# Layer 1's mixer of a two-layer trunk: query, key and output-gate projections as seven half-size products per pair, kept in DRAM, and four recurrences that run afterwards

## The chip, the core and the metric

The kernel runs on one core of one Trainium2 chip, as one program in one launch. The metric is the device time of that launch in microseconds (us). It counts the matmuls of the tensor engine (PE), its weight loads (PEld), the vector engine (DVE), the scalar engine (ACT), GpSimd (POOL) and the DMA queues, which are mostly issued by the sync engine (SP). Host work is not counted; numpy only lays the inputs out.

## The reference, cut to what matters

Two layers work on 1024 frames of width 1024. Layer 0 mixes with an attention and a pooling, layer 1 with gated linear attention, and each is followed by a feed-forward block. The change lies in layer 1's mixer (`odd_mixer`), which computes, with the batch left out:

```python
def odd_mixer(h, w_in, w_a2, b_a, o_gain, w_out):
    proj = h @ w_in
    q, k, v, r, a_low = jnp.split(proj, ...)        # 512, 512, 1024, 1024, 16 columns
    q = q.reshape(b, s, 4, 128) * 128 ** -0.5
    k = k.reshape(b, s, 4, 128)
    v = v.reshape(b, s, 4, 256)
    log_alpha = log_sigmoid(a_low @ w_a2 + b_a) / 16.0
    o = gated_linear_attention(q, k, v, log_alpha)
    o = rms_norm(o, o_gain).reshape(b, s, 1024)
    return (o * silu(r)) @ w_out

def step(state, inp):                               # once for each chunk of 64 frames
    q_c, k_c, v_c, decay_c = inp
    state = decay_c[..., None] * state + einsum('bchk,bchv->bhkv', k_c, v_c)
    return state, einsum('bchk,bhkv->bchv', q_c, state)
```

There are four heads, sixteen chunks, and a state of 128 x 256 for each head. `h` is `rms_norm(x, mix_norm_odd)`.

## The kernel before, in words

**Layout.** Activations lie transposed: 128 features on the partitions, 1024 frames along the free dimension, so `x` is eight tiles `x[0]` to `x[7]`. Every dense product is in three parts: each fp32 operand is split into a high and a low part (`hi`, `lo`, of type fp32r), and a product is hi x hi + hi x lo + lo x hi (`mm3`, lines 150 to 156, which the profile shows as L152, L154 and L156). A projection tile of 128 output features takes 8 input blocks x 2 halves of the frames x 3 = 48 matmuls of 128x512 (`linear`). A split is an ACT copy (L138) and a DVE subtraction (L139).

**What sets the order.** The order of PE is written out by hand: the program order of the matmuls is PE's order. The other engines and SP's DMA queue are put in order by the compiler, from a simulated time line with program order as priority. Within a recurrence a `Filler` hands out pieces of other generators, each `yield` saying how many us of PE work it stands for.

**The seven products.** The two feed-forward blocks (`ffn`) already use a scheme after Winograd and Strassen. Two projection tiles (a "pair") share 2x2 blocks of weights and activations; instead of eight products of half size there are seven (`Pair.P1` to `P7`, each 12 matmuls of 128x512, L937), and sums of weight halves (`sums`, L906 to L909) and of activation halves (`rsums`, L959 to L962, then `rblock`, which splits them) are made beforehand. `us` and `tm` are tiles for the pair's outputs and intermediate results. `scaled` (L965) multiplies by the norm's reciprocal.

**Layer 1's mixer before** (from L1187 on) uses no such scheme. While the last tiles of layer 0's down projection are added up, `Norm.add` (L255 to L271) splits `x[m]` into `h_hi`, `h_lo`, and head 0's key tile is projected between them (`onward`). Then, head by head:

- values `v_proj` (L1266 to L1268: 8 frame blocks of 24 matmuls of 128x256), evacuated by one ACT and one DVE instruction each (L1272, L1273);
- `q_proj`, `k_proj`, `r_proj` (`linear` again), and the gates (`gates`: one small matmul for each half, L1304, then ACT's Abs, Sigmoid, Ln, sixteen DVE scans, L1318, and Exp);
- `keys`: multiply by the decay, transpose on PE (L1334), split;
- `recur`: eight steps of two chunks. A step has six small matmuls for the state update (L1371 to L1373), DVE's new state (L1378), its split (L1380 on ACT, L1381 on DVE), and three matmuls that read the state of the step before (L1354 to L1356), whose result ACT copies out (L1358, L1359) and squares (L1361). One eighth of an `r_proj` tile fills each step;
- `gated`: root, reciprocal, eight scalings (ACT L1398, POOL L1400), PE transposes (L1409), product with the gate (L1412) and split (L1414, L1415), with the rest of the projections beside it;
- the output projection of that head is added to `x` (`accumulate`, L859), for the last head inside `ffn`.

Everything of the mixer stays in SBUF: `h` in the 16 tiles of `hpool`, `x` in eight of the 11 slots of `xpool`. Weights pass through one raw tile (`wraw`) and two pairs of split tiles (`whi`, `wlo`) in `wpool`. The four PSUM tags `lin`, `z`, `t` and `d` have two banks each.

## Time and profile before

| what | value |
|---|---|
| time, median of 3 runs | 2246.44 us |
| lowest and highest | 2243.03 and 2246.78 us |
| the profiled execution's own time | 2246.21 us |
| span in the profile, first to last instruction | 2244.2 us |
| mean granted PE clock | 0.998 |
| layer 1's mixer, from the last head-0 key products to the first product of its `ffn` | 1128.15 to 1530.80 us of the span |
| HBM traffic | 159.98 MB read, 42.99 MB written |

"Busy" is the time in which an engine has at least one instruction under way. Matmuls overlap in the array, so the mean duration of a 128x512 matmul (about 0.39 us) is not the time that it costs: that is the distance from one start to the next, which comes out of a stretch of the trace divided by the matmuls in it. "Idle before" of a group is what its engine waited ahead of it, and an arrow names the instruction that ended the wait.

### The profile page before, as it was taken

The numbers are of one execution on the slowest core, as the hardware profiler recorded it, in microseconds if no ns is written. First come the engines' busy times: TensorE is split into PE (matmuls) and PEld (weight loads), VectorE is DVE, ScalarE is ACT, GpSimd is POOL, SyncE is SP. The second block draws the span as 40 slices with busy tenths as digits, with TensorE's granted clock in tenths as the row PEclk, the third lists the DMA queues.
The fourth block names the chain that finished last, engine by engine and source line by source line (L and its number), as shares of the span: only waits on it lengthen the run. The fifth ranks groups of instructions, "written<-read, shape, count | busy, mean of one in ns | idle before, by whom it ended". The sixth has DMA issues, their size and how long they took to land.

```text
span 2244.2 us, 27677 instructions
## 1 busy us (share of the span) xinstructions
PE 2208.7 (98%) x10648; PEld 1815.5 (81%) x10648; DVE 1590.4 (71%) x2239; ACT 1010.5 (45%) x1488; POOL 229.4 (10%) x184
## 2 busy tenths in 40 slices
PE   8999989999999999999999999999999999999999
PEld 7888868788888888888887878887888888888887
DVE  5687788788888889554546555547888888885543
ACT  6666666454444444221256263537544444442210
POOL 2230120000000001421000000001000000013210
PEclk9999999999999999999999999999999999999999
DMA  4132441433333336421101111105333333364312
GB/s 149 52 106 81 118 140 51 146 100 112 107 106 108 113 113 225 160 98 53 31 20 48 29 47 38 48 29 164 91 108 107 113 109 103 109 226 148 110 40 75
DMA packets 71908, 220.50 MB, mean 98 GB/s; under 512 B 8400, under 2 KB 11088, under 8 KB 71776
## 3 DMA queue, kind: packets, MB, share of 16 engines
q1 hardware_dynamic: 64576, 203.00, 28.1%
q0 software_dynamic: 7200, 15.73, 3.9%
q8 instruction: 84, 1.38, 0.3%
q14 instruction: 48, 0.39, 0.1%
HBM read 159.98 MB, written 42.99 MB: 90 GB/s over the span
## 4 chain that ended last, share of the span: by engine, by line
PE 88%; DVE 4%; ACT 3%; DMA 2%; issue 1%; SPq 0%; POOL 0%; DVEq 0%; ACTq 0%; POOLq 0%
PE lin L937 15%; PE z L937 10%; PE lin L152 6%; PE lin L154 5%; PE lin L156 5%; PE t L937 5%; PE d L937 5%; PE z L152 4%; PE z L154 4%; PE z L156 4%; PE t L152 3%; PE t L154 3%; PE t L156 2%; PE d L154 2%; PE d L152 2%; PE d L156 2%
## 5 line engine op out<-in xcount | busy, mean ns | idle before, releaser
L138 ACT CAST whi<-wraw 128x1024 fp32r<-128x1024 f32 (+2 forms) x102 | 104.2, 1023 | 341.1 <-PE d L154 182.0
L139 DVE TENSOR_TENSOR wlo<-wraw,whi 128x1024 fp32r<-128x1024 f32 (+1 forms) x88 | 128.5, 1461 | 44.5 <-ACT whi L138 43.8
L1010 ACT ACTIVATE c<-u,prm 128x1024 f32<-128x1024 f32 x88 | 109.3, 1244 | 106.2 <-DVE u L965 89.8
L1174 POOL TENSOR_TENSOR act<-a,act 128x1024 fp32r<-128x1024 f32 x40 | 105.6, 2647 | 268.8 <-ACT act L1173 254.5
L152 PE MATMUL lin<-h_hi,whi 128*128 128x512 f32 x304 | 118.2, 427 | 7.2 <-ACT whi L138 6.1
L937 PE MATMUL d<-T,a 128*128 128x512 f32 x480 | 115.4, 389 | 0.0
L1011 DVE SCALAR_TENSOR_TENSOR c<-u,prm,c 128x1023 f32<-128x1023 f32 x88 | 112.2, 1277 | 3.7 <-ACT c L1010 3.6
L1013 DVE SCALAR_TENSOR_TENSOR c<-u,prm,c 128x1022 f32<-128x1022 f32 x88 | 113.7, 1294 | 0.1
L908 POOL DMA_DIRECT2D s<-s x40 | 34.4, 859 | 762.4 <-ACT s12h L916 619.1
L154 PE MATMUL lin<-h_lo,whi 128*128 128x512 f32 x304 | 108.7, 395 | 1.7 <-DVE h_lo L262 1.7
L965 DVE TENSOR_TENSOR u<-u,rstd_bc 128x512 f32<-128x512 f32 x160 | 109.3, 683 | 0.3
L156 PE MATMUL lin<-h_hi,wlo 128*128 128x512 f32 x304 | 108.3, 395 | 0.0
L859 DVE TENSOR_TENSOR x<-x,t 128x512 f32<-128x512 f32 x93 | 63.5, 683 | 59.7 <-PE t L156 59.7
L937 PEld LDWEIGHTS d<-T,a 128*128 128x128 f32 x480 | 90.1, 188 | 18.7
L937 PE MATMUL z<-blk,s34h 128*128 128x512 f32 x320 | 100.9, 397 | 0.0
L937 PE MATMUL z<-blk,s12h 128*128 128x512 f32 x320 | 100.9, 396 | 0.0
L937 PE MATMUL t<-blk,whi 128*128 128x512 f32 x320 | 99.6, 392 | 0.0
L937 PE MATMUL lin<-blk,whi 128*128 128x512 f32 x320 | 99.5, 392 | 0.0
L859 DVE TENSOR_TENSOR x<-x,d 128x512 f32<-128x512 f32 x93 | 63.4, 682 | 50.9 <-PE d L156 50.9
L937 PE MATMUL lin<-T,s12h 128*128 128x512 f32 x320 | 99.3, 391 | 0.0
L937 PE MATMUL lin<-T,s34h 128*128 128x512 f32 x320 | 99.3, 391 | 0.0
L859 DVE TENSOR_TENSOR x<-x,z 128x512 f32<-128x512 f32 x78 | 53.3, 683 | 60.0 <-PE z L156 60.0
(444 smaller groups left out, 6336.7 us busy)
## 6 DMA issues: line engine op xcount, KB each, us to landing
wraw<-in_wup SPq DMA_DIRECT2D x44, 512.0 KB, 3.6
act<-c SPq DMA_DIRECT2D x44, 512.0 KB, 2.6
wraw<-in_wdn SPq DMA_DIRECT2D x44, 512.0 KB, 4.0
raw_g<-in_wup SPq DMA_DIRECT2D x40, 512.0 KB, 3.7
a<-act SPq DMA_DIRECT2D x40, 512.0 KB, 4.4
s<-in_wup SPq DMA_DIRECT2D x40, 256.0 KB, 2.6
s<-s POOLq DMA_DIRECT2D x40, 256.0 KB, 4.2
xs<-x SPq DMA_DIRECT2D x16, 512.0 KB, 3.4
```

The source lines that it names most:

```text
L138: S.copy(hi[:, cs], raw[:, cs])
L139: (eng or V).tensor_tensor(lo[:, cs], raw[:, cs], hi[:, cs].bitcast(F32), op=ALU.subtract)
L152: PE.matmul(out[i], wh, ah[i], start=first, stop=False)
L154: PE.matmul(out[i], wh, al[i], start=False, stop=False)
L156: PE.matmul(out[i], wl, ah[i], start=False, stop=last)
L859: V.tensor_tensor(x[m][:, cs], x[m][:, cs], pss[m][i], op=ALU.add)
L937: PE.matmul(ps, w, m, start=first and k == 0 and n == 0, stop=k == 3 and n == 2, skip_group_check=True)
L965: V.tensor_tensor(dst, dst, rstd_bc[:, cs], op=ALU.mult)
L1010: S.activation(c, u, AF.Identity, scale=pcol(b + 2), bias=pcol(b + 3))
L1011: V.scalar_tensor_tensor(c[:, 1:], u[:, :T - 1], pcol(b + 1), c[:, 1:], op0=ALU.mult, op1=ALU.add)
L1013: V.scalar_tensor_tensor(c[:, 2:], u[:, :T - 2], pcol(b), c[:, 2:], op0=ALU.mult, op1=ALU.add)
L1174: G.tensor_tensor(t[1], a32, t[0].bitcast(F32), op=ALU.subtract)
```

## The change

Layer 1's mixer is put in a new order, and most of its projections are computed in another way.

- `winograd(...)` is taken out of `ffn` as a function, with the same operations, and is used a second time.
- `norm` becomes a `NormBlocks`: each `x[m]` is stored to DRAM (`xs`), and split in four blocks by half of the frames; `x[0..3]` are scaled in place. With `by_dma=False` the squares are added by DVE.
- Head 0's key (still with `linear_b` in `onward`) and query stay plain, 48 matmuls each. The other three keys, three queries and the eight tiles of `r` are seven pairs.
- First come head 0's values, with `rsums` and `rblock` (16 sums, 16 splits of 128x512) beside them, then head 0's query, the gates of heads 0 and 1, the second half of the frames of head 2's and head 3's values, the gates of heads 2 and 3, all of head 1's values; then the seven pairs in a row, with `keys`, `queries` and `r_gate` beside them.
- All results go to DRAM tiles (`qd`, `kd`, `vhd`, `vld`, `rd`, `ed`) and are fetched again by `fetch_half` and `fetch_r` when a recurrence needs them. `x` leaves its slots and is loaded again by `reload_x` in the second recurrence.
- Then the four recurrences run one after another. Their fillers are: in recurrence 0 the first half of head 2's values (four pieces, one of them ahead of it), in recurrence 1 that of head 3's, in recurrences 2 and 3 the output projection of heads 0 and 1 together (16 pieces, two of them ahead), and then that of head 2. Head 3's is left to `ffn`, as before.

The loops around the pairs and the recurrences, cut:

```diff
-    norm = Norm(C_MIXO, lambda: slot(F32, "nacc"), lambda: slot(F32, "nsq"), V)
+    norm = NormBlocks("m", C_MIXO, lambda: slot(F32, "nacc"), lambda: slot(F32, "nsq"), by_dma=False)
...
+    PAIRS = ([(wok[1], wok[2]), (wok[3], woq[1]), (woq[2], woq[3])]
+             + [(wor[2 * hd], wor[2 * hd + 1]) for hd in range(GH)])
+    w = winograd(gp, norm, lambda i: PAIRS[i], us, tm, t1=lambda: slot(R32, "T1"))
...
+    for k in range(4):
+        w.rsums(k)
+        for n in ("T4", "T2", "T3", "T1"):
+            w.rblock(n, k)
+        next(v)
...
+    v = v_proj(3, SECOND, w3, lambda a: (slot(R32, "vst"), w.a22), v_store(3), vtags)
+    next(v)
+    w1 = v_weights(1)
+    next(v)
+    gates((2, 3), ("lin", "z"), [(w.raw_g, w.s34), (w.s12, lz)])
+    run(v)
+    v = v_proj(1, [*SECOND, *FIRST], w1, lambda a: (slot(R32, "vst"), slot(R32, "vst")), v_store(1), vtags)
+    for _ in range(4):
+        next(v)
+    loads = (w.load_g, w.load_a, w.load_s4)
+    for ld in loads:
+        ld(0)
+    w.split_a22()
+    w.sums(0)
...
+    run(v)
...
+    for i in range(N):
+        nx, further = i + 1 < N, i + 2 < N
+        if i == 0:
+            p = w.Pair(0)
+            p.P1()
+        ua, ug = p.ua, p.ug
+        if i == 1:
+            ks[1], ks[2] = keys(1, us[0]), keys(2, us[1])
+            next(ks[1])
...
+        p.P5()
+        if nx:
+            w.sums(i + 1)
+            w.split_a11(i + 1)
...
+        p.P4()
+        p.D21()
...
+            p = w.Pair(i + 1)
+            p.P1()
+        pq.P3()
...
+        if i >= 3:
+            for f, u in enumerate((ua, ug)):
+                r_gate(i - 3, f, u)
...
+    fetch_half(0, 0)
+    fetch_half(0, 1)
+    fl = Filler()
+    fl.add(early(2, wf))
+    fl.fill(2.6)
+    nxt = {}
+    o0 = recur(0, fl, 10.4, {3: lambda: fetch_half(1, 0), 4: lambda: nxt.update(w=v_weights(3)),
+                             5: lambda: (fetch_half(1, 1), fetch_r(0))})
+    g0 = gated(0, *o0)
+    next(g0)
+    fl.add(early(3, nxt["w"]))
+
+    def in1(j):
+        if j == 2:
+            mixt[0] = next(g0)
+        elif j == 3:
+            fetch_half(2, 0)
+            ow[0] = [out_w(0, hpool, ("h", "h"), nb=16), out_w(1, hpool, ("h", "h"), nb=16)]
+        elif j == 4:
+            run(g0)
+        elif j == 5:
+            fetch_half(2, 1)
+            fetch_r(1)
+            reload_x()
+        elif j == 6:
+            ow[1] = [out_w(2), out_w(3)]
+
+    o1 = recur(1, fl, 16.0, {j: (lambda j=j: in1(j)) for j in range(NT)})
+    g1 = gated(1, *o1)
+    next(g1)
+    mixt[1] = next(g1)
+    run(g1)
+    fl.add(outputs_of(ow[0] + ow[1], mixt[0] + mixt[1]))
+    fl.fill(5.2)
...
+    keep(fl)
+    o2 = recur(2, fl, 18.0, {j: (lambda j=j: in2(j)) for j in range(NT)})
+    g2 = gated(2, *o2)
+    next(g2)
...
+    o3 = recur(3, fl, 20.0, {j: (lambda j=j: in3(j)) for j in range(NT)})
+    g3 = gated(3, *o3)
+    next(g3)
+    del fl.drain
+    fl.drain()
+    o = outputs_of(ow[2], mixt[2])
     for _ in range(4):
-        next(rr)
...
+        next(o)
+    mixt[3] = next(g3)
+    for _ in range(4):
+        next(o)
+    run(g3)
+    run(o)
```

The functions that these lines call, where they are new or different:

```diff
+    def gates(hds, tags, tiles):
+        for hd, tag, (l1, l2) in zip(hds, tags, tiles):
...
+                PE.matmul(gp_, gin["w"][:, hd * GDK:(hd + 1) * GDK], gin["a"][:, cs], start=True, stop=True)
+                S.activation(l1[:, cs], gp_, AF.Abs, bias=ba)
+                V.tensor_scalar(l2[:, cs], gp_, ba, 0.0, op0=ALU.add, op1=ALU.min)
+        for f in (AF.Sigmoid, AF.Ln):
+            for l1, _ in tiles:
+                S.activation(l1, l1, f)
...
+        for hd, (l1, _) in zip(hds, tiles):
+            S.activation(l1, l1, AF.Exp, scale=1.0 / TAU)
+            S.activation(decs[hd], decs[hd], AF.Exp, scale=1.0 / TAU)
+            dma(ed[hd], l1)
...
+    def early(hd, wt):
+        return v_proj(hd, FIRST, wt, lambda a: (ring("vh")(), ring("vl")()), v_store(hd), ltags)
...
+    def outputs_of(ws, acts):
+        for m in range(KT):
+            sl = slice(m * P, (m + 1) * P)
+            for cs in HALVES:
+                ps = bank(next(ltags))
+                for k, (wk, ak) in enumerate(zip(ws, acts)):
+                    mm3([ps], (wk[0][:, sl], wk[1][:, sl]), ([ak[0][:, cs]], [ak[1][:, cs]]),
+                        k == 0, k == len(ws) - 1)
+                yield 0.65 * len(ws)
+                V.tensor_tensor(x[m][:, cs], x[m][:, cs], ps, op=ALU.add)
+
+    def keep(fl):
+        fl.drain = lambda: None
```

`ffn` keeps its own calls and takes the functions from `winograd`. The scan, the state update and the read of a recurrence are the same instructions as before, with other operand tiles.

More of the change, by code (lines that the diff above doesn't have):

```diff
@@ L865, in accumulate, with winograd @@
                 after(m)
-    def ffn(layer, nm, after, ow, mixt, onward=None):
-        ev = ExitStack()
-        up = ev.enter_context(tc.tile_pool(name=f"up{layer}", bufs=1, reuse_waits="tile"))
+    def winograd(up, nm, wt, us, tm, t1=lambda: hpool.tile([P, T], R32, tag="h", name="blk")):
         T0, T1 = HALVES
@@ new lines, in onward, with dt @@
+    def onward(load):
+        return linear_b(load(wok[0]), lambda cs, ps: V.tensor_tensor(
+            k0[0][:, cs], ps, rstd_bc[:, cs], op=ALU.mult), "lin", late=late)
+    ffn(0, n0, lambda m: norm.add(m, x[m]), ws, [mix[k] for k in last], onward)
+    def dt(name):
+        return dram.tile([P, T], F32, tag=name, name=name)
+    qd, kd, vhd, vld = ({(hd, a): dt(f"{n}{hd}_{a}") for hd in range(GH) for a in range(2)}
+                        for n in ("qd", "kd", "vhd", "vld"))
+    rd = {(hd, f): dt(f"rd{hd}_{f}") for hd in range(GH) for f in range(2)}
@@ new lines, in r_gate @@
+    def r_gate(hd, f, u):
+        S.activation(u, u, AF.Silu)
+        dma(rd[hd, f], u)
+    k0.append(w.s34)
+    v0to = [(w.s12h, w.s12l), (w.s34h, w.s34l)]
+    v = v_proj(0, range(NT), ahead, lambda a: v0to[a], v_store(0), itertools.cycle("td"))
+    next(v)
+    norm.stats("z")
+    next(v)
+    next(v)
+    norm.spread(itertools.repeat("z"))
+    for f in late:
+        f()
+    dma(raw0["k"], w.s34)
+    for k in range(4):
[3 more added lines that the diff above has]
+        next(v)
@@ new lines, in trunk_kernel @@
+    qw = [w.s12h, w.s12l]
+    qraw = wpool.tile([P, T], F32, tag="wraw", name="wraw", bufs=1)
+    dma(qraw, woq[0])
+    next(v)
+    w.split(*qw, qraw)
+    run(v)
+    g = gate_inputs()
+    next(g)
+    q32 = slot(F32, "q32")
+    q = linear_b(tuple(qw), lambda cs, ps: V.tensor_tensor(q32[:, cs], ps, rstd_bc[:, cs], op=ALU.mult), "z")
+    for _ in range(4):
+        next(q)
+    run(g)
+    for _ in range(3):
+        next(q)
+    lz = slot(F32, "l2")
+    gates((0, 1), ("lin", "td"[0]), [(w.raw_g, w.s34), (w.s12, lz)])
@@ L1346, in recur, with fetch_r @@
+    sr = {}
+    def fetch_r(hd):
+        for f in range(2):
+            sr[hd, f] = op.tile([P, T], F32, tag="r", name="r32", bufs=2)
+            dma(sr[hd, f], rd[hd, f])
+    def recur(hd, fl, us_, at):
+        dec = decs[hd]
+        oraw = []
         ss = small.tile([P, NT], F32, tag="ss", name="ss")
```

450 lines of the change are left out of this document (261 added, 189 removed).

## The prediction

> **What bounds the kernel now.** I read the page first, then the chain of waits, then the windows of layer 1's mixer, then the groups of ACT and DVE inside it.
>
> ```profile
> span 2244.2 us, 27677 instructions
> PE 2208.7 (98%) x10648; PEld 1815.5 (81%) x10648; DVE 1590.4 (71%) x2239; ACT 1010.5 (45%) x1488; POOL 229.4 (10%) x184
> PE 88%; DVE 4%; ACT 3%; DMA 2%; issue 1%; SPq 0%; POOL 0%; DVEq 0%; ACTq 0%; POOLq 0%
> ```
>
> PE is busy in 98% of the span and is 88% of the chain that ends last. So a PE instruction less is time saved, as long as PE finds its operands, and a PE wait added is time lost. The windows say where PE waits today (columns: length, then busy time and count of PE, PEld, DVE, ACT, POOL, then clock, DMA share, GB/s).
>
> ```profile
> 1106.00:1128.15 22.15, 22.15 (x96) 17.81 (x96) 20.23 (x24) 13.10 (x14) 0.62 (x1) 1.00 0.00 0
> 1128.15:1135.15 7.00, 5.86 (x26) 4.43 (x25) 7.00 (x8) 5.20 (x6) 0.33 (x1) 1.00 0.00 0
> 1135.15:1162.90 27.75, 27.75 (x214) 26.75 (x213) 7.34 (x14) 10.35 (x22) 0.00 (x0) 1.00 0.01 1
> 1237.00:1240.80 3.80, 1.63 (x8) 0.98 (x6) 3.77 (x6) 0.88 (x1) 0.13 (x1) 1.00 0.18 22
> 1240.00:1245.00 5.00, 4.20 (x12) 3.34 (x13) 5.00 (x19) 1.05 (x1) 0.00 (x0) 0.68 0.38 107
> 1284.60:1307.80 23.20, 23.11 (x122) 16.51 (x122) 17.02 (x37) 15.97 (x44) 0.00 (x0) 1.00 0.16 46
> 1516.80:1530.80 14.00, 13.36 (x65) 10.43 (x64) 5.46 (x9) 11.53 (x21) 1.85 (x4) 1.00 0.44 151
> 1530.80:1547.10 16.30, 13.46 (x51) 10.02 (x50) 14.89 (x22) 10.86 (x16) 0.88 (x1) 0.90 0.42 145
> 1128.15:1530.80 402.65, 398.38 (x2222) 332.15 (x2221) 219.34 (x413) 199.67 (x379) 8.24 (x21) 1.00 0.14 41
> ```
>
> In 402.65 us PE idles 4.3 us. A recurrence (1284.60 to 1307.80 is head 1's) is filled without a gap: 23.2 us.
>
> **The change, part by part.** First what a matmul costs, from three stretches with one kind of work: one `r` tile (48 matmuls, counted by their weight loads), one pair of the feed-forward block (84), four value steps.
>
> ```profile
> 1318.70:1329.60 10.90, 10.90 (x49) 8.96 (x48) 2.44 (x4) 3.42 (x4) 0.00 (x0) 1.00 0.18 48
> 1661.30:1680.70 19.40, 19.40 (x85) 15.77 (x84) 16.79 (x21) 8.84 (x10) 0.86 (x1) 1.00 0.38 109
> 1267.20:1278.70 11.50, 11.50 (x98) 11.50 (x97) 1.93 (x4) 1.90 (x4) 0.00 (x0) 1.00 0.01 1
> ```
>
> *Products.* Fourteen plain tiles go, 14 x 10.90 = 152.6 us; seven pairs come, 7 x 19.40 = 135.8 us. That is **-16.8 us**. Values, outputs, transposes, gate matmuls and the recurrences' own matmuls stay the same in number.
>
> *Waits that go.* Head 0's output products wait today for a query's evacuation, and the clock falls after it:
>
> ```profile
> PE z L152 <- DVE q L1228: 2.2, 1, 2.2
> PE d L152 <- DVE x L859: 2.1, 1, 2.1
> ```
>
> 2.2 us and (1 - 0.68) x 5 = 1.6 us, **-3.8 us**: that place no longer exists. At the end of the mixer (1516.80 to 1547.10) PE idles 0.6 + 2.8 us and loses 0.10 x 16.3 = 1.6 us of clock, 5.0 in all, while DVE is busy 14.89 of 16.30 us with the last head's gating, weight splits and the first sums at once. In the new order 16 pieces of output products lie behind that gating's start, so DVE has it done earlier; the splits remain. Bounds 0 and -5.0; I take **-3.5**.
>
> *The blocks of the norm.* Eight `x[m]` get two half splits in place of a whole one. DVE had 20.23 busy of 22.15 us before 1128 and is full to 1135. Two 0.747 in place of one 1.28 is 0.2 us for each, 1.7 in all, partly hidden: **+0.5** (0 to 3).
>
> ```profile
> L305 DVE SCALAR_TENSOR_TENSOR blk<-x,prm,blk 128x512 fp32r<-128x512 f32 x16 | 11.6, 747 | 1.0 <-ACT blk L304 1.0
> L962 DVE SCALAR_TENSOR_TENSOR x<-x,prm 128x512 f32<-128x512 f32 x4 | 3.0, 742 | 0.0
> L917 DVE TENSOR_TENSOR T<-x,T 128x512 fp32r<-128x512 f32 x12 | 8.0, 675 | 0.0
> L1273 DVE SCALAR_TENSOR_TENSOR vl<-t,rstd_tok,vh 128x256 fp32r<-128x256 f32 x16 | 7.7, 483 | 32.6 <-ACT vh L1272 32.6
> ```
>
> *Sums beside head 0's values.* For each k DVE gets four sums and four splits, about 3 x 0.742 + 5 x 0.675 = 5.6 us, 22.4 in all, on top of 7.34 in a stretch of 27.75 us. 29.7 us is 2 too many, but durations overlap a little. If a value tile's evacuation (0.483) queues behind a k's 5.6 us, PE waits for its bank. **+1** (0 to 6).
>
> *Gates to first pair.* The second pair of heads' gates use tiles `raw_g` and `s12`, which the first pair's weights need next. In between lie Abs, Sigmoid, Ln, the scans, Exp, a store, the sums and a split:
>
> ```profile
> L1305 ACT ACTIVATE l<-lin,prm 128x512 f32<-128x512 f32 x8 | 5.2, 686 | 5.1 <-PE lin L1304 5.1
> L1307 ACT ACT_TABLE_LOAD x4 | 5.1, 1283 | 0.1
> L1308 ACT ACTIVATE l<-l 128x1024 f32<-128x1024 f32 x4 | 4.2, 1062 | 0.0
> L1314 DVE TENSOR_TENSOR l<-l,l 128x1008 f32<-128x1008 f32 x4 | 4.8, 1204 | 0.1
> L1318 DVE TENSOR_TENSOR_SCAN l<-ones,l 128x64 f32<-128x64 f32 x64 | 12.3, 266 | 0.0
> act<-c SPq DMA_DIRECT2D x44, 512.0 KB, 2.6
> L138 ACT CAST whi<-wraw 128x1024 fp32r<-128x1024 f32 x29 | 30.3, 1046 | 77.1 <-PE z L154 42.9 <-PE lin L154 15.9 <-DMA wraw<-in_wov 8.9
> L139 DVE TENSOR_TENSOR wlo<-wraw,whi 128x1024 fp32r<-128x1024 f32 x28 | 34.1, 1219 | 21.3 <-ACT whi L138 21.3
> ```
>
> ACT: 4 x 0.686 + 2 x 1.283 + 4 x 1.062 = 9.6; DVE: 2 x (1.2 + 16 x 0.266) = 10.9; Exp 1.3 + 2 x 1.06 = 3.4; store 2.6; two half sums 1.4; split 1.05 + 1.22: 30.2 us. PE meanwhile has two value steps, eight more, and `P1` (19.40 / 7 = 2.8): 10 x 2.88 + 2.8 = 31.6 us. It fits by 1.4, before ten evacuations and two weight splits take ACT and DVE for up to 7 us each. `P5` waits **+2** (0 to 9), and `P6` to `P3` are queued behind it. The sum that goes through POOL's DMA queue is needed only by `P7`, three products later.
>
> *Seven pairs.* In the feed-forward block a pair leaves PE no gap with DVE at 16.79 of 19.40; here the convolutions fall away, `keys`, `queries` and Silu come in. **+0.5** (0 to 4). The DRAM round trips I cost at nothing: some 27 MB out and 27 back in about 390 us is 140 GB/s beside 41 now, and the 151 GB/s row has a DMA share of 0.44. The cover is a distance of a whole stage; without it one late tile is 2.6 out and 3.6 to 5.9 back.
>
> ```profile
> wraw<-in_wor SPq DMA_DIRECT2D x8, 512.0 KB, 3.6
> x<-xs SPq DMA_DIRECT2D x16, 512.0 KB, 5.9
> SPq L127 <- DVE wlo L139: 260.7, 25, 63.3
> ```
>
> *The recurrences.* Today each step has 1.36 us of filler (10.90 / 8); its own PE part is (23.20 - 10.90) / 8 = 1.5 us. ACT and DVE need for a step:
>
> ```profile
> L1380 ACT CAST sh<-state 128x256 fp32r<-128x256 f32 x64 | 25.7, 402 | 12.6 <-DVE state L1378 5.9 <-DVE state L1376 5.4
> L1358 ACT COPY oraw<-t 64x256 f32<-64x256 f32 x32 | 11.7, 366 | 14.4 <-PE t L1356 14.1
> L1361 ACT ACTIVATE junk<-oraw 128x256 f32<-128x256 f32 x32 | 13.4, 417 | 0.8
> L1361 ACT ACTIVATION_READ_ACCUMULATOR junk<-oraw 128x1 f32 x32 | 6.0, 187 | 0.0
> L1378 DVE SCALAR_TENSOR_TENSOR state<-state,dec,d 128x256 f32<-128x256 f32 x60 | 28.7, 479 | 18.4 <-PE d L1373 15.4
> L1381 DVE TENSOR_TENSOR sl<-state,sh 128x256 fp32r<-128x256 f32 x64 | 27.0, 422 | 1.5 <-ACT sh L1380 0.2
> L1398 ACT ACTIVATE oraw<-oraw,ss 128x256 f32<-128x256 f32 x16 | 6.8, 498 | 1.1 <-DVE ss L1394 1.1
> L1414 ACT CAST mh<-r 128x512 fp32r<-128x512 f32 x14 | 8.3, 614 | 0.4 <-DVE r L1412 0.4
> ```
>
> ACT 2 x 0.402 + 2 x 0.366 + 0.417 + 0.187 = 2.15 us, DVE 2 x (0.479 + 0.422) = 1.8. So a step without filler takes at least ACT's 2.15 and at most the 2.9 of a filled one. Recurrence 0 has filler in three of eight steps (2.88 each): the other five lose 0.65 to 1.4 each, and the last read, with nothing ahead of it, about 1; a long piece lets ACT catch up. **+3.5** (2 to 8). Recurrence 1's pieces all fall in its first four steps. ACT there has 8 x 2.15 + 8 x 0.498 for both gatings' scalings + 8 x 0.614 + 4 x 1.046 for output weights + 4 x 0.475 for values + 1.6 for the root = 33.8 us, against PE's 8 x 1.5 + 4 x 2.88 = 23.5 and both gatings' transposes. The gating of head 1 stands bare before the output products, so PE waits most of that difference of 10 us, less its transposes: **+7** (4 to 15). The clock falls once after it, **+1.6** (0 to 5). Recurrences 2 and 3 carry seven 2.8 us pieces each, PE 31.6 against ACT's 17 to 24: only their last reads stand bare, **+2** (1 to 5).
>
> A word on that clock. The Trainium skill ("TensorE: Matmul & The Clock Gate", Part 1: The HAM clock gate) says that the clock is halved after an idle window of about 3.4 us and returns after about as long of sustained work. The rows agree in the length, but not in the condition: here 3.80 us with PE busy 1.63 were enough. By the page, steps that are merely thin cost no clock, and the sum below would be 2238.6.
>
> *Sum:* -16.8 - 3.8 - 3.5 + 0.5 + 1 + 2 + 0.5 + 3.5 + 7 + 1.6 + 2 = **-6.0**. The profiled execution took 2246.21 us (2.0 around its span), 0.2 below the median of the three runs, 2246.44. Forecast: **2240 us**.
>
> **The rivals.** *All hidden:* every new wait at its lower bound (0 + 0 + 0 + 0 + 2 + 4 + 0 + 1 = 7), the end's 5.0 gone: -18.6, 2228 us. For it: DVE and ACT idle much of the mixer (219 and 200 of 402.65 us). Against: they idle elsewhere than where the new work is.
>
> *Even:* recurrences 0 and 1 at 4 to 6 above my values. 2245 us.
>
> *Thin recurrences cool the clock (slower).* Nine steps in recurrences 0 and 1 have PE busy 1.5 of 2.15 to 2.9 us, 52 to 70%; the fall was seen after 43%. It decides from there: at half clock a step's PE part is 3.0 us, over ACT's 2.15 by 0.85, so 9 x 0.85 = 7.6 us; three more half-clock stretches of 1.6 are 4.8, and recurrence 1 with its weight splits in the way goes to its upper bound, 8 more. -6.0 + 20.4 = +14.4: 2261 us.
>
> *The SP queue holds the pairs back (slower).* A load waits in it up to 63.3 us for its tile today, and nothing behind it matters. Now stores of keys, queries and values stand behind such loads. If each pair starts 2 us late, +14 for seven: 2254 us.
>
> *It doesn't do what it says:* the seven products could cost as much as eight only if a pair took 21.8 us; the row says 19.40. I give it nothing.
>
> **How the numbers follow.** The forecast, 2223 to 2241: 0.38; all hidden 0.12; even 0.20; cooled clock 0.18; SP queue 0.12. Faster by over 0.2% (4.5 us, about what a measurement of this kernel can tell from no change) is 0.50, within it 0.20, slower 0.30. The range 2224 to 2262 takes in the bounds and leaves out about 2 in 10.
>
> **What would show it.** Right: seven pairs at 19.4 to 19.6 us; the first `P5` waiting under 4 us on `s12`; recurrence 0 at 23 to 26 us, recurrence 1 with its gating near 34, recurrences 2 and 3 at 31 to 34; clock below 1 at one place. Wrong: pairs that wait for raw weights or `us`, waits of PE on fetched tiles, clock at half through recurrence 0 or 1, or PE waits beside head 0's values over 6 us.

## The result: slower, and the profile after

| | before | after |
|---|---|---|
| median of the runs timed together, us | 2244.82 (4 runs, 2243.03 to 2246.78) | 2280.02 (4 runs, 2276.27 to 2285.89) |
| ratio to before, 95% interval | | 1.0159 (1.0134 to 1.0184) |
| profiled execution, its span, us | 2246.21, 2244.2 | 2285.89, 2284.2 |
| mean granted clock | 0.998 | 0.984 |

The kernel became 1.6% slower; the forecast was 0.3% faster, and 2280 lies above the range. The changed kernel was timed a second time (last experiment): 2278.57 us, 1.0141 (1.0127 to 1.0154). In e16_warm2 below one execution of five took 7853 us at a granted clock of 0.27, and one of the kernel before beside it 2768 us at 0.73; the medians and ratios leave both out.

The engines' line of the page after the change:

```profile
PE 2214.9 (97%) x10564; PEld 1822.2 (80%) x10564; DVE 1650.6 (72%) x2333; ACT 1034.5 (45%) x1544; POOL 236.6 (10%) x191
```

PE has 84 products fewer (10648 before) and is busy 6 us *longer*. The windows of the mixer say how (length, then busy time and count of PE, PEld, DVE, ACT, POOL, then clock, DMA share, GB/s):

```profile
1132.10:1574.70 442.60, 402.58 (x2138) 333.35 (x2137) 279.21 (x501) 220.33 (x430) 15.09 (x28) 0.94 0.50 169
1132.10:1144.95 12.85, 8.04 (x26) 5.61 (x25) 12.85 (x18) 7.52 (x11) 0.95 (x1) 0.77 0.17 71
1186.94:1249.21 62.27, 52.02 (x389) 51.15 (x389) 37.99 (x108) 38.13 (x51) 1.38 (x5) 0.89 0.47 161
1249.21:1395.97 146.76, 140.73 (x623) 115.30 (x622) 90.08 (x121) 53.93 (x73) 5.16 (x6) 0.98 0.58 190
1357.20:1376.60 19.40, 19.40 (x86) 15.91 (x85) 12.60 (x18) 7.26 (x9) 0.86 (x1) 1.00 0.53 161
1398.90:1425.60 26.70, 24.29 (x145) 18.17 (x144) 16.18 (x37) 17.00 (x49) 0.00 (x0) 0.87 0.97 345
1425.60:1466.10 40.50, 34.17 (x201) 27.78 (x201) 25.26 (x52) 30.65 (x77) 3.91 (x8) 0.84 0.91 336
1466.10:1478.20 12.10, 8.32 (x26) 5.58 (x24) 6.69 (x9) 2.86 (x4) 0.00 (x0) 0.84 0.66 224
1478.20:1574.70 96.50, 90.90 (x442) 69.62 (x442) 62.53 (x116) 44.02 (x118) 3.69 (x8) 0.98 0.17 55
1574.70:1591.00 16.30, 15.47 (x68) 12.42 (x67) 14.77 (x22) 11.72 (x15) 0.88 (x1) 1.00 0.75 247
```

The first row is the whole mixer, the next eight are: the last head-0 key products, the values of heads 2, 3 and 1, the seven pairs, one pair alone, recurrence 0, recurrence 1 with head 1's gating, the first output products, and the rest; the last row is the start of the feed-forward block. Against 402.65 us before, the mixer is 40 us longer. PE idles 40.0 us where it idled 4.3: 36 us more. Its busy time rose by 4.2 us although 16.8 us of products went: some 21 us are the same products taking longer. Nearly all of that is the low clock: PE's busy time times what the granted clock lacks of 1.00, summed over windows of 1 us, is 21.2 us, and 1.7 us before. 36 + 21 - 17 = 40. On the average of this mixer, each microsecond in which PE stood still came with another 0.6 us of low clock.

What PE waited for in the mixer (in total, times, longest):

```profile
PE t L1574 <- ACT sh L1605: 7.5, 8, 2.0
PE t L1360 <- DVE k L1354: 5.7, 1, 5.7
PE lin L155 <- DVE blk L306: 4.8, 2, 4.6
PE d L1596 <- DVE r L1635: 4.1, 4, 1.4
PE t L1278 <- ACT whi L139: 3.9, 1, 3.9
PE t L1279 <- DVE wlo L140: 3.3, 1, 3.3
PE t L1279 <- DVE s34l L908: 3.1, 1, 3.1
PE t L1632 <- ACT oraw L1623: 2.5, 1, 2.5
PE lin L153 <- ACT whi L139: 2.4, 1, 2.4
```

No single wait carries the loss. There are six places: the recurrences, at their reads (L1574) and at state updates that need the bank `d` which a gating still holds (L1596), transposes of head 0's keys (L1360), the last blocks of the norm (L306), value weights (L1278, L1279), head 1's gating (L1632) and output weights (L153). The forecast had terms for the first, third and fifth of these.

### The profile page after: what moved, and what is told of

It is laid out like the page before. It is cut to its first block, busy times and chain, and to the rows that moved or that the text cites. A ratio compares the mean times of both kernels' runs of the same rounds, so it can differ in the third digit from the quotient of the medians.

```text
span 2284.2 us, 27985 instructions
## 1 busy us (share of the span) xinstructions
PE 2214.9 (97%) x10564; PEld 1822.2 (80%) x10564; DVE 1650.6 (72%) x2333; ACT 1034.5 (45%) x1544; POOL 236.6 (10%) x191
## 5 line engine op out<-in xcount | busy, mean ns | idle before, releaser
L926 PE MATMUL d<-T,a 128*128 128x512 f32 x564 | 135.8, 390 | 0.0
L954 DVE TENSOR_TENSOR u<-u,rstd_bc 128x512 f32<-128x512 f32 x188 | 129.8, 690 | 0.9
L926 PEld LDWEIGHTS d<-T,a 128*128 128x128 f32 x564 | 105.9, 188 | 22.0
L926 PE MATMUL z<-blk,s34h 128*128 128x512 f32 x376 | 118.0, 395 | 0.0
L926 PE MATMUL lin<-T,s34h 128*128 128x512 f32 x376 | 116.5, 391 | 0.0
L926 PE MATMUL lin<-T,s12h 128*128 128x512 f32 x376 | 116.1, 390 | 0.0
L926 PE MATMUL lin<-blk,whi 128*128 128x512 f32 x368 | 115.4, 395 | 0.0
L907 ACT CAST whi<-wraw 128x1024 fp32r<-128x1024 f32 x46 | 48.5, 1054 | 125.8 <-DMA wraw<-in_wup 104.3
L995 DVE TENSOR_TENSOR u<-tm,z 128x512 f32<-128x512 f32 x47 | 32.3, 688 | 99.3 <-PE z L926 99.3
L926 PEld LDWEIGHTS z<-blk,s34h 128*128 128x128 f32 x376 | 70.5, 188 | 17.2 <-DVE u L985 0.6
```

The lines of the kernel that those rows point to most:

```text
L926: PE.matmul(ps, w, m, start=first and k == 0 and n == 0, stop=k == 3 and n == 2, skip_group_check=True)
L954: V.tensor_tensor(dst, dst, rstd_bc[:, cs], op=ALU.mult)
```

## Experiments

Every kernel is the changed one with the edit shown. A table first. "Time" is the ratio to the kernel before, minus 1.0150 (the mean of the changed kernel's two ratios), times 2246 us; its interval is 3 to 5 us to either side, and the changed kernel's own mean is no surer than 3 us. By time alone, e1, e2, e7, e8, e9, e12, e13 and e16 can't be told from the changed kernel. "Mixer" is read from one profile each: from the start of the 24 last head-0 key products to the first feed-forward product in bank `d`, 408.1 us before and 446.7 and 446.0 in the changed kernel's two profiles; the column is against 446.4. It leaves out what happens ahead of the mixer, where the same code ended anywhere from 1125 to 1132 us.

| run | edit | median, us | ratio (95%) | time | mixer |
|---|---|---|---|---|---|
| e1_values | value weights' low halves on GpSimd | 2282.1 | 1.0158 (1.0140 to 1.0175) | +1.8 | +4.8 |
| e2_blocks | sums behind the norm's blocks | 2278.5 | 1.0151 (1.0130 to 1.0172) | 0 | 0 |
| e3_keys0 | head 0's keys a pair earlier | 2275.5 | 1.0123 (1.0109 to 1.0137) | -6.1 | -2.6 |
| e4_warm | 252 idle products | 2293.1 | 1.0202 (1.0188 to 1.0215) | +11.7 | +13.4 |
| e5_noscan | no running sums in the gates | 2273.7 | 1.0124 (1.0109 to 1.0139) | -5.8 | -6.2 |
| e6_spread | gates in pieces | 2275.2 | 1.0132 (1.0115 to 1.0149) | -4.0 | -6.3 |
| e7_fill | output products into recurrence 1 | 2276.0 | 1.0138 (1.0114 to 1.0162) | -2.7 | -2.4 |
| e8_nox | no reload of x | 2277.6 | 1.0143 (1.0123 to 1.0164) | -1.6 | +0.3 |
| e9_late | sums behind the spread of the norm | 2279.6 | 1.0144 (1.0130 to 1.0158) | -1.3 | -1.2 |
| e10_comb | e3, e6, e7, e9 | 2264.7 | 1.0080 (1.0067 to 1.0093) | -15.7 | -15.9 |
| e11_now1 | head 1 with head 3's weights | 2287.4 | 1.0180 (1.0166 to 1.0195) | +6.7 | +7.6 |
| e12_act | a copy of the read on VectorE | 2285.1 | 1.0158 (1.0138 to 1.0178) | +1.8 | +3.7 |
| e13_now1b | head 1 with head 2's weights | 2278.0 | 1.0137 (1.0120 to 1.0154) | -2.9 | -2.7 |
| e14_fill2 | e7, and values into recurrence 0 | 2268.6 | 1.0098 (1.0084 to 1.0111) | -11.7 | -9.5 |
| e15_comb2 | e3, e6, e9, e14 | 2260.6 | 1.0066 (1.0054 to 1.0079) | -18.9 | -16.9 |
| e16_warm2 | 124 idle products, bare places only | 2282.7 | 1.0161 (1.0140 to 1.0182) | +2.5 | not read |
| e17_again | none | 2278.6 | 1.0141 (1.0127 to 1.0154) | | |
| e18_comb3 | as e15, splits of the sums later | 2260.7 | 1.0069 (1.0054 to 1.0084) | -18.2 | -20.7 |

### The values of heads 2, 3 and 1

The first idea was that these weights pass one raw tile, whose VectorE split stands behind the gates' running sums.

```diff
-v = v_proj(2, SECOND, v_weights(2), ...)
+v = v_proj(2, SECOND, v_weights(2, eng=G), ...)
...
-            w.split(hi, lo, raw)
+            S.copy(hi, raw); (eng or V).tensor_tensor(lo, raw, hi.bitcast(F32), op=ALU.subtract)
```

> The six splits of the value weights of heads 2, 3 and 1 ahead of the pairs write their low halves on GpSimd and not on VectorE, so that the one raw tile no longer waits behind the scans. Theory (late operands): in the changed kernel PE is busy 51.75 us of the 62.00 between 1187 and 1249 and waits three times there, 3.1, 3.9 and 3.3 us, each followed by a stretch at half the granted clock; the three waits go and most of the low clock with them, 10 to 16 us, so about 2265 to 2270 where the changed kernel has 2280. Rival (memory traffic: the loads themselves land late, beside the stores of the values, DMA share 0.48 in that stretch): within 3 us of 2280. Rival (the thin recurrences and their clock are all of the loss): within 3 us of 2280 also, with the three waits gone and the time given back at the pairs.

It gained nothing. The waits of PE in its values and its first pair:

```profile
PE t L1278 <- ACT whi L139: 4.8, 1, 4.8
PE d L1278 <- DVE a L1285: 3.2, 1, 3.2
PE lin L926 <- ACT tm L976: 2.6, 1, 2.6
```

The wait on head 3's weights became one on the evacuation of a value (L1285), which is queued behind the same running sums; that on the high copy of head 1's weights stayed, that on their low half fell from 3.3 to 2.0 us; and a new one came in the first pair. So VectorE's split alone isn't the cause. Two runs then each took one suspect away, the running sums (first) and the turns of the raw tile:

```diff
-            for c in range(NCH):
+            for c in range(0):
```

> Leaves out the 64 running sums of the gates (16 for each head), so the decays are wrong; all else stays. In the run with the splits on GpSimd the waits at 1200, 1216 and 1221 stayed, with other names. Theory (queues held by the gates: VectorE is held by 16 to 32 running sums in a row, ScalarE by the exponential that waits for them, the load queue by the store behind that): without the running sums the stretch of values from 1187 to 1249 loses less than 5 us in place of 15, and the kernel takes 2264 to 2271. Rival (memory traffic, loads of weights late beside the stores of values): the waits stay: 2276 to 2284. Rival (values themselves too dense for ScalarE and VectorE): same, 2276 to 2284.

```diff
-v = v_proj(2, SECOND, v_weights(2), ...)
+v = v_proj(2, SECOND, w2 := v_weights(2), ...)
...
-    w1 = v_weights(1)
+    w1 = w2
```

> Leaves out the two loads and splits of head 1's value weights again, now with head 2's weights in their place (they stay in their tiles; the output is wrong). Theory (the raw tile's turns are behind the waits of 3.9 and 3.3 us): the values lose only the 3.3 us before and its low clock, 7 to 9 us less: 2271 to 2275, or 2275 to 2278 if the first pair's weight sums are then late. Rival (the gates hold ScalarE and VectorE, so the evacuations are late instead): 2279 to 2284.

For each, the window of the values and that of the first 20 us of the pairs. In the changed kernel the second one is:

```profile
1249.21:1269.21 20.00, 20.00 (x90) 16.31 (x89) 11.43 (x16) 6.44 (x10) 0.86 (x1) 1.00 0.42 113
```

e5_noscan:

```profile
1183.33:1233.33 50.00, 47.60 (x388) 46.81 (x389) 26.84 (x44) 34.47 (x48) 1.38 (x5) 1.00 0.57 197
1233.33:1253.33 20.00, 16.16 (x61) 12.45 (x60) 8.04 (x10) 5.32 (x7) 0.86 (x1) 0.87 0.41 113
```

then e13_now1b:

```profile
1180.31:1232.04 51.73, 48.63 (x389) 48.25 (x389) 33.09 (x102) 35.29 (x48) 1.38 (x5) 0.97 0.44 157
1232.04:1252.04 20.00, 15.25 (x60) 11.68 (x59) 10.61 (x14) 5.42 (x7) 0.86 (x1) 0.91 0.49 149
```

The values fall from 62.27 to 50.00 and 51.73 us. The changed kernel waits there 3.1 us on head 3's weights (`s34l`) and 3.9 and 3.3 us on head 1's. e13_now1b, without head 1's turns, loses the last two and keeps the 3.1 us; e5_noscan loses the first, and 1.4 and 0.9 us are left of the others. So the waits on head 1's weights need both: a turn of the one raw tile (load, ScalarE copy, split) and gates that hold ScalarE and VectorE while the turn is due. For head 3's, only the gates' part is shown. Then more than half is given back: in the first 20 us of the pairs 61 and 60 products run where the changed kernel has 90, 30 x 0.23 = 7 us. ScalarE of e13_now1b at that place, by time (start, length, and in brackets its idle time and what ended it):

```profile
1245.77 1.04 ACT L907 CAST whi<-wraw 128x1024 fp32r<-128x1024 f32 x1 [7.08 <-DMA wraw<-in_woq]
...
1247.66 0.58 ACT L976 COPY tm<-lin 128x512 f32<-128x512 f32 x1
```

The copy of `A` (L976), which PE needs for `P7`, stands behind the high copy of the *third* pair's weights (`woq[2]`), which PE needs only two pairs later, and that waits 7.08 us for its load. e5_noscan has the same order there, with 7.15 us. It isn't the first pair's weight sums, as I had expected, but ScalarE's queue. (The Trainium skill, "PSUM — Partial Sum Buffer", "Engine vs sequencer instructions", says that this queue is strictly first in, first out; the rows agree, with these 7.08 us.)

The run ahead of this one had used head 3's weights:

```diff
-    w1 = v_weights(1)
+    w1 = w3
```

> Leaves out the two loads and splits of head 1's value weights (its values are made with head 3's weights, so the output is wrong): two fewer turns of the one raw tile, 1 MB and 4 passes of 1024 columns less. Theory (the raw tile's turns, each a load and a split, are the chain behind the waits of 3.9 and 3.3 us at 1213 and 1217): both go with the low clock behind them, the values are 7 to 10 us shorter, 2270 to 2274, or 2276 if the first pair's weight sums are then late. Rival (ScalarE and VectorE are full with the gates, whatever is loaded): 2278 to 2282.

It took 7 us more, and says little: the first pair's splits write those tiles, so PE waited 10.2 us for `s12h` (L907) in the middle of the values.

A remedy that keeps the work, gates in pieces of four running sums behind each value step:

```diff
                 V.tensor_tensor_scan(rev, ones[:, 0:64], rev, 0.0, op0=ALU.mult, op1=ALU.add)
+                if c % 4 == 3:
+                    yield
...
+    for _ in v:
+        steps(ga, 2)
```

> The same work in another order: the running sums of the gates in pieces of 4, two pieces behind each step of values, the exponentials and the stores of the gates last; heads 0 and 1 over the values of heads 2 and 3, heads 2 and 3 over those of 3 and 1. Theory (queues held by the gates): most of the 15 us come back, 2266 to 2272. Rival (VectorE is full in this stretch whatever the order): 2278 to 2284, the waits now on the evacuation of the values or on the first pair's sums. Rival (memory traffic): 2278 to 2284, the waits on the weights' loads.

```profile
1185.04:1241.66 56.62, 49.75 (x388) 48.88 (x389) 39.37 (x111) 39.08 (x52) 1.37 (x5) 0.94 0.53 177
1241.66:1261.66 20.00, 20.00 (x90) 16.38 (x89) 10.21 (x13) 5.94 (x9) 0.86 (x1) 1.00 0.36 113
```

The values are 5.7 us shorter and the pairs start clean. The time, 2275, stays short of the expected 2266 to 2272. One long wait is left, on the high copy of head 1's weights (it shows in the last run's waits below).

### The last blocks of the norm

VectorE in the changed kernel, by time:

```profile
1133.87 0.76 DVE L306 SCALAR_TENSOR_TENSOR blk<-x,prm,blk 128x512 fp32r<-128x512 f32 x1
...
1135.13 0.76 DVE L949 SCALAR_TENSOR_TENSOR x<-x,prm 128x512 f32<-128x512 f32 x1
1135.79 1.30 DVE L140 TENSOR_TENSOR wlo<-draw,whi 128x1088 fp32r<-128x1088 f32 x1
...
1139.52 0.76 DVE L306 SCALAR_TENSOR_TENSOR blk<-x,prm,blk 128x512 fp32r<-128x512 f32 x1
```

Between two blocks that PE waits for lie 5 us with three of the sums (L949 to L951) and two splits of value weights; the first of each is shown. Two orders were tried; first the sums behind the last block:

```diff
+        with tc.issue_after(norm.sub.ins):     # the last block's split
             w.rsums(k)
             for n in ("T4", "T2", "T3", "T1"):
                 w.rblock(n, k)
```

> The sums and differences of x for the seven products, and the splits of these, are queued on VectorE behind the last block of the norm. Theory (late operands): the last head-0 key products took 12.85 us in the changed kernel against 7.2 us before, with three waits of 5.2 us in all on the blocks; they fall back and the clock stays up: 4 to 7 us less than 2280, about 2274. Rival (VectorE is full there, the sums only come later): the four sums and sixteen splits are then late for the first pair's products and the wait shows there; within 2 us of 2280.

Two windows, the first 13 us and all up to the query's products, and what PE waited for:

```profile
1125.58:1138.58 13.00, 12.52 (x78) 10.82 (x77) 12.95 (x18) 6.77 (x10) 0.95 (x1) 1.00 0.11 43
1125.58:1167.07 41.49, 36.58 (x238) 32.59 (x236) 34.19 (x54) 24.83 (x46) 0.95 (x1) 0.92 0.18 66
```

```profile
PE z L291 <- DVE nsq L284: 4.4, 1, 4.4
```

In the first 13 us PE now runs 78 products where the changed kernel ran 26 in 12.85, but then the statistics of the norm wait 4.4 us for a tile that VectorE writes behind the sums. The same stretch of the changed kernel is no longer, so nothing is gained:

```profile
1132.06:1173.01 40.95, 36.14 (x238) 32.75 (x236) 32.89 (x50) 25.83 (x48) 0.95 (x1) 0.92 0.20 76
```

Then behind that tile, with the splits' low halves on GpSimd:

```diff
+        with tc.issue_after(norm.dgi.ins):     # the tile that spreads the norm
...
-            split(t[:, T0], t[:, T1], src)
+            S.copy(t[:, T0], src)
+            G.tensor_tensor(t[:, T1], src, t[:, T0].bitcast(F32), op=ALU.subtract)
```

> The sums of x for the seven products wait on VectorE until the tile that spreads the norm is written, and the low halves of their sixteen splits are made on GpSimd. With the sums only behind the last block, the 7.3 us lost at the last head-0 key products went and 4.6 + 1.9 + 1.4 us came in the statistics of the norm behind them. Theory (an order that puts the sums ahead of what PE waits for): now neither is there, 5 to 8 us less than 2280, about 2274. Rival (VectorE is full over the whole stretch): the sums are late for the evacuation of the values or for the first pair: 2278 to 2284.

```profile
1127.53:1164.33 36.80, 34.10 (x237) 31.22 (x236) 30.82 (x35) 19.19 (x37) 20.27 (x13) 1.00 0.15 59
```

```profile
PE lin L1329 <- ACT alow L1321: 3.1, 1, 3.1
```

This place is 4.15 us shorter, and 3.1 us come back at the gates' products. I took GpSimd's queue for the cause, and e15_comb2 below cleared the tile on VectorE: the wait stayed at 2.9 us. e18_comb3 moved the splits instead, and it stayed too. Its ScalarE rows show why:

```profile
1172.46 0.56 ACT L1319 CAST alow<-t 16x512 fp32r<-16x512 f32 x1
1176.75 1.04 ACT L139 CAST whi<-wraw 128x1024 fp32r<-128x1024 f32 x1 [3.73 <-DMA wraw<-in_wov]
1177.70 0.57 ACT L1319 CAST alow<-d 16x512 fp32r<-16x512 f32 x1
```

The low-rank gate's copy from bank `d`, which PE had filled by 1172.9, stands behind a high copy of value weights that waits 3.73 us for its load: the same mechanism as at the first pair. In e9_late and e15_comb2 both of the gate's copies stand behind such a copy, which waits 2.76 and 2.63 us.

### Head 0's keys

```diff
         if i == 2:
             run(ks[3])
+            k32 = slot(F32, "k32")
+            dma(k32, raw0["k"])
+            ks[0] = keys(0, k32)
+            next(ks[0])
```

(and the same four lines leave `i == 3`)

> The loads of head 0's raw keys and of its gate, and their product, are issued one pair earlier (after head 3's keys are transposed). Theory (late operands): the wait of 5.7 us of the transposes on the product of keys and gate at 1326 and the low clock behind it (13.31 us busy of the 19.00 from 1322 to 1341, clock 0.82) go: 6 to 8 us less than 2280, about 2273. Rival (the queue of the loads is what is late, whatever the place): the load is queued behind the stores of heads 1 to 3 there as well, and the wait stays or moves to the query products: within 2 us of 2280.

The wait of 5.7 us is gone, and yet the pairs take 145.26 us in place of 146.76, for two new waits appear:

```profile
PE lin L926 <- ACT tm L976: 4.1, 2, 2.1
```

The first, in the first pair, is the one seen above: the copy stands behind the third pair's weights, which wait 6.33 us for their load. The second, at 1341 us, stands behind other work of ScalarE (the activation of `r`, a query, a split). The mixer is 2.6 us shorter; the time says 6.1, with an interval that takes in both.

### The recurrences

Four runs on what binds recurrences 0 and 1: the clock, ScalarE, traffic, filler.

```diff
+            if hd < 2:
+                idle(6)        # PE.matmul of constants, twice in each step; 20 three times round g1
```

> Adds idle products (128x128, on constants, read by nobody): 12 in each of the 8 steps of recurrences 0 and 1 and 60 around head 1's gating, 252 in all, some 27 us of PE time at the 0.109 us pitch of 128 columns; nothing else is changed. Theory (clock): the recurrences are slow since their short stops halve the granted clock (0.87 to 0.89, 0.76 in the gating); with the array kept busy the clock is 1.00 there and the time falls by 5 to 10 us, to about 2272, although work is added. Theory (late operands: PE waits there for ScalarE and VectorE): products that fall into the waits cost nothing and those outside cost their 0.109 us: 2280 to 2290. Neither: if PE itself were the bound there, all 27 us are added, 2307.

```diff
-            S.copy(oj[64:128], po[64:128, GDV:512])
+            V.tensor_copy(oj[64:128], po[64:128, GDV:512])
```

> In the recurrences the second of the two copies out of the read bank moves from ScalarE to VectorE (32 copies of 64x256 in all four heads). Theory (ScalarE is the bound of steps without filler: two copies of the state, two of the read and a square each): steps without filler are 0.3 us shorter, about 16 of them, with some clock: 4 to 8 us less than 2280. Rival (the chain from the update over VectorE, ScalarE and VectorE to the read is the bound, whichever engine is freer): 2278 to 2283. Rival (traffic, DMA share 0.9 in recurrences 0 and 1): 2278 to 2283 too.

```diff
-            dma(x[m], xs[m])
+            G.memset(x[m], 0.0)
```

> Leaves out the 8 loads of x (4 MB) in recurrence 1, and clears those tiles on GpSimd in their place, so the residual is missing from the output. Theory (memory traffic bounds recurrence 1 and head 1's gating, the output weights land behind x): 8 to 13 us less, 4 MB at the 320 GB/s of that stretch being 13 us: 2267 to 2272. Theory (PE waits there for ScalarE and VectorE alone): 2278 to 2282, the wait for the split of the last output weight stays.

```diff
         elif j == 4:
             run(g0)
+            fl.add(outputs_of(ow[0], mixt[0]))
...
-    fl.add(outputs_of(ow[0] + ow[1], mixt[0] + mixt[1]))
+    fl.add(outputs_of(ow[1], mixt[1]))
```

> Head 0's output products (96 products of 512 columns, some 22 us) are moved from the recurrences 2 and 3 into recurrence 1 and the gating of head 1, with their weights and the reload of x earlier; head 1's follow in recurrences 2 and 3 at a lower rate. The accumulation is parted, so 16 more additions of 128x512 fall to VectorE. Theory (in recurrences 0 and 1 PE waits for ScalarE and VectorE with nothing to do in between): the 18 us lost from 1426 to 1478 become half, and the rest of the head is shorter by as much: 2268 to 2275. Rival (memory traffic: DMA share 0.9 there, 345 GB/s; the earlier loads crowd out the heads' operands): 2280 to 2290. Rival (ScalarE and VectorE are the bound of the recurrences and have no room for 16 more additions): 2278 to 2286.

And, once e7_fill had shown recurrence 0 still bare:

```diff
+    w3 = [load_split(wov[2][c], hpool, ("h", "h"), nb=16) for c in range(2)]
-    fl.add(early(2, wf))
+    fl.add(early(2, wf), early(3, w3))
```

> As the run with head 0's output products in recurrence 1, and besides, head 3's first four value steps (some 12 us of products) move from recurrence 1 into recurrence 0, with their weights in four free tiles, loaded ahead of recurrence 0. Theory (missing filler): the bare last steps of recurrence 0 are covered too, 5 to 7 us less than with recurrence 1 filled alone: 2268 to 2272. Rival (memory traffic: 1 MB more is loaded where DMA share is 0.96, the heads' operands come late): 2276 to 2284. Rival (VectorE and ScalarE, which evacuate the values): 2275 to 2280.

One window serves for all, from the last pair product to head 3's gating. The changed kernel:

```profile
1395.97:1556.11 160.14, 142.01 (x746) 108.69 (x744) 98.74 (x195) 93.10 (x244) 7.60 (x16) 0.91 0.55 197
```

e4_warm, e12_act, e8_nox, e7_fill and e14_fill2:

```profile
1391.89:1564.74 172.85, 162.53 (x997) 134.63 (x996) 99.72 (x195) 94.23 (x244) 7.59 (x16) 0.96 0.51 183
```

```profile
1394.79:1557.82 163.03, 145.74 (x745) 109.61 (x744) 111.80 (x227) 80.49 (x210) 5.94 (x13) 0.92 0.54 194
```

```profile
1391.92:1552.68 160.76, 145.24 (x746) 111.05 (x745) 98.44 (x195) 93.16 (x244) 14.75 (x24) 0.87 0.49 170
```

```profile
1397.74:1551.73 153.99, 141.50 (x746) 107.14 (x744) 106.37 (x211) 93.26 (x244) 7.59 (x16) 0.92 0.58 205
```

```profile
1390.31:1540.66 150.35, 138.94 (x746) 106.41 (x745) 106.18 (x211) 92.38 (x244) 7.59 (x16) 0.93 0.58 210
```

*Clock:* e4_warm's clock rises from 0.91 to 0.96, and the stretch is 12.7 us longer. The 252 products are 27 us at their pitch, so some 15 us of them cost nothing: PE's idle time fell by 7.8 us, from 18.1 to 10.3, and its busy time rose by 20.5, some 7 us less than the products added. So the better clock gave something back, but not what the products cost. What the low clock alone costs there, no run shows. e16_warm2 put 124 of them in the bare places alone:

```diff
+            if hd < 2 and j >= 6:
+                idle(8)
```

> Idle products (128x128) in the bare places alone: 16 in each of the last two steps of recurrences 0 and 1 and 60 around head 1's gating, 124, some 14 us at the 0.109 us pitch. Theory (low clock is a good part of the loss there: granted clock 0.87 to 0.89, 0.76 in the gating): 3 to 7 us less than 2280. Theory (missing filler; PE waits, and the clock only follows): they cost nothing or little where they fall into waits: 2279 to 2286.

The time is 2.5 us more, which its interval doesn't tell from nothing; the 3 to 7 us less of its first theory aren't seen. *ScalarE:* with 13 us less on ScalarE (80.49 for 93.10) and 13 more on VectorE the stretch is no shorter; a case in which both have less to do wasn't run. *Traffic:* with 4 MB less it is no shorter either (160.76 us). One wait does go: that of 2.4 us on the output weights (L153), so the loads of `x` had been in their way; but the clock is 0.87 in place of 0.91, and the length stays. *Filler:* the same 746 instructions of PE in 150.35 us, 9.8 less, though VectorE has 16 more additions. So these 10 us come from the new order of the fillers and of what they load: e7_fill and e14_fill2 also fetch weights and `x` earlier, and the wait on the output weights is gone in both. The filler alone isn't told apart from that. The 11.4 us in which PE still idles there are not taken apart further.

### Together

e10_comb has the edits of e3, e6, e7 and e9 as they are above.

> Four edits together: the sums behind the spread of the norm, the running sums of the gates in pieces, head 0's keys one pair earlier, head 0's output products in recurrence 1. Against the changed kernel the last three gave about 6, 8 and 5 us alone, the first is expected to give 5 to 8. Theory (separate late operands, each with its own price): the gains add, 2253 to 2259. Rival (one late operand hides another, above all the first pair's weight sums behind a shorter stretch of values): half of it, 2264 to 2270. Neither reaches the 2245 of before, since the last waits of recurrences 0 and 1 stay.

e15_comb2 has e14's in place of e7's, and

```diff
-        G.memset(zz, 0.0)
+        V.memset(zz, 0.0)
```

> The four edits together with head 3's values in recurrence 0, and the clearing of the gates' tile on VectorE, since GpSimd's splits stood ahead of it (3.3 us of wait of the gates' products). Against 2264.7 of the four edits: theory (each late operand has its own price): 3 us from the clearing and 4 to 6 from recurrence 0, 2255 to 2259. Rival (they hide each other): 2262 to 2267. The kernel before has 2245; if all causes were found and mended it would be at 2235 to 2240, and the rest of this run over that is the waits on head 1's weights and what is left of the recurrences.

e18_comb3 takes that line back and moves twelve splits:

```diff
-            for n in ("T4", "T2", "T3", "T1"):
-                w.rblock(n, k)
+            w.rblock("T4", k)
...
     run(g)
+    for n in ("T2", "T1", "T3"):
+        for k in range(4):
+            w.rblock(n, k)
```

> As the run with all edits (2260.6), but the tile of the gates is cleared on GpSimd again, and twelve of the sixteen splits of x's sums (all but the blocks T4) are issued behind the low-rank gate's copies. Theory (the splits stand ahead of these copies on ScalarE): the waits of 2.9, 2.2 and 1.1 us of the gates' products, the values and the transposes on ScalarE's low-rank copies go: 2253 to 2258. Rival (those copies wait for the values' evacuation whatever stands there, or the splits are then late for the first pair): 2258 to 2264.

e15_comb2 and e18_comb3 differ by noise in time. The mixer of e18_comb3 and the largest of its waits:

```profile
1127.70:1549.30 421.60, 394.49 (x2138) 325.96 (x2137) 287.44 (x504) 218.46 (x428) 39.81 (x44) 0.96 0.51 176
```

```profile
PE t L1279 <- ACT whi L139: 5.2, 1, 5.2
PE t L1592 <- ACT sh L1623: 5.0, 4, 1.8
PE lin L1329 <- ACT alow L1321: 2.8, 2, 1.8
```

Alone, e3, e6, e9 and e14 shorten the mixer by 2.6, 6.3, 1.2 and 9.5 us, 19.6 in all; together by 16.9 and 20.7. So they add. (By time, e10_comb lies in its rival's range and e15_comb2 between the two, since the expectations had set each gain higher than the mixer shows it.) About half of the 38 us is accounted for, and no version reached the kernel before. Last, the changed kernel once more, without an edit:

> The changed kernel as it is, once more. If its first median of 2280.0 (ratio 1.0159) was drawn high by what happens ahead of the mixer, where its profiled run is 3 to 7 us later than the variants: 2274 to 2279, ratio 1.012 to 1.0145, and 3 to 4 us of each variant's gain are no gain. If not: 2279 to 2284, ratio 1.015 to 1.017.

The second timing of the changed kernel, 2278.57 us and 1.0141, lies at the upper end of the first range. The two ratios differ by 4 us, which their intervals allow; the table counts from the mean of both. Its mixer (446.0 us) repeats the first (446.7), and it began at 1128.4 in place of 1132.1. So 4 of the 40 us by which the two spans differ lie ahead of the mixer and are no effect of the change.

## Why the prediction was wrong

Its terms, with what the rows above give. In the right column, what a stretch took is set against its products at the pitch of the prediction's rows.

| term | predicted (bounds) | measured |
|---|---|---|
| products | -16.8 | -16.8: a pair took 19.40 |
| wait on the query | -3.8 | -3.8: that place is gone |
| end of the mixer | -3.5 (-5.0 to 0) | -4.2: idle 0.8 of 16.30, clock 1.00 |
| blocks of the norm | +0.5 (0 to 3) | +5.9: 12.85 for 7.00 with 26 products |
| sums beside head 0's values | +1 (0 to 6) | about 0 |
| gates to first pair | +2 (0 to 9) | 0: no wait of `P5` |
| values of heads 2, 3, 1 | no term | +15.3: 62.27 for 16 x 2.88 + 0.9 |
| seven pairs, round trips | +0.5 (0 to 4) | +7.5: 146.76 for 135.8 and 3.5 of transposes |
| recurrence 0 | +3.5 (2 to 8) | +6.1: 26.70 for 8 x 1.5 + 3 x 2.88 |
| recurrence 1 and gating | +7 (4 to 15) | +13.5: 40.50 for 12 + 4 x 2.88 + 3.5 |
| first output products | no term | +6.6: 12.10 for 24 x 0.231 |
| clock, once | +1.6 (0 to 5) | within the stretches above |
| recurrences 2 and 3 | +2 (1 to 5) | +7.5: idle 5.6, clock 0.98 of 96.50 |

The right column sums to +37.6, and the mixer with what follows is 36.1 us longer in the spans (2284.2 - 1132.1 against 2244.2 - 1128.2).

**Right:** the products, the wait on the query, the end of the mixer, and the first `P5`.

**The step that failed most is a missing term.** "PE meanwhile has two value steps, eight more, and `P1` ...: 10 x 2.88 + 2.8 = 31.6 us" took the value steps as cover for the gates, at full speed, and asked only when the *pair* gets its tiles. The value steps need their own weights through one raw tile, past the same queues. I had named this ("before ten evacuations and two weight splits take ACT and DVE for up to 7 us each") and charged it to `P5` alone. The term stood at nothing and came to 15.3 us. For head 1's weights e5_noscan and e13_now1b show that the gates and the raw tile together make the wait.

**Blocks of the norm:** durations were right, the order wrong. I counted the sums behind the blocks; VectorE's order has some of them ahead. The two terms together were +1.5 and came to 5.9. e2_blocks shows that its order alone doesn't mend it, since VectorE's work there is then late elsewhere.

**Round trips "at nothing":** the amount was right (28 MB more written, 32 MB more read, for 27 each way). The cover was a distance of a whole stage, and head 0's keys didn't have it, as the load queue and VectorE of the changed kernel show, by time:

```profile
1325.14 0.32 SPq L1256 DMA_DIRECT2D e<-ed  x1
...
1331.09 1.23 DVE L1354 TENSOR_TENSOR k<-k,e 128x1024 f32<-128x1024 f32 x1 [2.38 <-DMA e<-ed]
```

The gate `e` is fetched less than 6 us ahead of the product that needs it, and the transposes stand right behind that. The text gave the price of a late tile, 3.6 to 5.9 us; the wait was 5.7. e3_keys0 removes it, and 4.1 us come back as two waits on ScalarE's queue.

**Recurrences:** the mechanism was right, the sizes too small. Recurrence 0 and recurrence 1 lie within their bounds, both in the upper half; by the prediction's own signs they are too long, 26.70 us for 23 to 26 and 40.50 for "near 34". Recurrences 2 and 3 lie above their bound, 7.5 for at most 5: their last reads wait 3.3 us, and 2.3 us more are updates that wait for the bank `d` of the gating before (L1596), which had no term. The output products behind recurrence 1 had no term either, since I counted their weight splits as ScalarE time in recurrence 1 and not as a wait of their own.

**The clock** was charged once, 1.6 us. It fell at most of the places above, and cost 21 us over the mixer. The rival "thin recurrences cool the clock" saw its mechanism; two windows of recurrence 0, whose clock was 1.00 up to there, show the fall:

```profile
1416.00:1419.50 3.50, 2.67 (x11) 1.41 (x9) 2.42 (x6) 2.56 (x9) 0.00 (x0) 0.91 1.01 270
1419.50:1423.00 3.50, 2.95 (x10) 1.55 (x9) 2.07 (x6) 2.04 (x7) 0.00 (x0) 0.50 0.97 321
```

Its price there isn't settled: e4_warm lifts the clock and gets some 7 us of PE's busy time back, but the products that do it cost more. How much of the low clock only fills time that PE would have waited stays open. "The SP queue holds the pairs back" didn't come: the only load that PE waits for in the pairs of the changed kernel is head 0's. And no rival had PE's waits spread over six places.

The Trainium skill ("TensorE: Matmul & The Clock Gate", "Why this matters for your kernels") advises to leave no gap of over some 3 us between bursts of products. Here the rows differ in the condition: the clock went to 0.50 at the end of 3.50 us with PE busy 2.67 of them, and the one wait in them is of 0.83 us.
